# One matmul stream, eight column tiles: input scaled but not yet shifted, and w times shift added to the result

## The chip, the core and the metric

The kernel runs on one core of a Trainium2 chip. TensorE multiplies, VectorE (DVE), ScalarE (ACT) and GpSimd (POOL) do elementwise work, SyncE (SP) issues the loads, and 16 DMA engines carry them. The metric is device time of one execution in microseconds; the median of three executions of the kernel before is 2745.55 us.

## The reference, cut to what matters

The network is three transformer layers on 512 positions of width 2048. The change lies at the start of the first, where the input is normalised, scaled and shifted by vectors that depend on a condition `c`, and then multiplied by a wide matrix:

```python
sh_x, sc_x, gt_x = jnp.split((jax.nn.silu(c) @ w_ada[l] + b_ada[l])[:, None, :], 3, axis=-1)
h_x = rms_norm(x, norm_g[l]) * (1 + sc_x) + sh_x
h_c = rms_norm(hc, norm_g[l]) * (1 + sc_c) + sh_c
px = split_cols(h_x @ w_in[l])
pc = split_cols(h_c @ w_in[l])
```

`x` has 512 rows and the context `hc` 256. `w_ada` is 2048 x 6144 in float32: its scale and its shift third are 16.8 MB each. Everything is float32, and a product `h @ w` is made of three passes over operands that are split into a high and a low part.

## The kernel before

**Layout.** Activations stand transposed: 16 tiles of 128 features (k = 0 to 15) by 512 positions. One column tile of a weight is 128 output columns; it takes 16 x 3 matmuls of 128 x 512 (lines 491 to 493: high x high, high x low, low x high), and, where the context is projected too, 16 x 3 of 128 x 256 (496 to 498).

**The stream.** All weights go through one list of units of 256 KB, `self.units`, in the order in which TensorE uses them. A unit is either a quarter of a column tile (four k; called a quarter below) or one of 64 pieces of a third of `w_ada`. Two units make a pair, and a pair takes a slot of 512 KB. `loads` (in `stream`) issues a pair as soon as a slot of its kind is free. While the unit's number is below `EARLY` = 160, slots come from a ring of six (two `wr`, two `pt`, two pairs of `P`); after that from two `wr`. A quarter's unit is cast to the high part by ScalarE (line 554), the low part is the remainder, mostly by GpSimd (564); this uses the raw data up. A piece of `w_ada` is used raw: four pieces make a group of four matmuls on TensorE (667), and only when the group has run are their shares of the slots free. A slot is free when both of its units are used.

**The modulation stage (`block1`).** The pieces go by blocks of four k: the 16 pieces of the scale of block b, then the 16 of its shift. When a block's 16 pieces are in, its PSUM bank is copied (305 or 303), transposed by four small matmuls (641), and put into the table `modv` (647, 656). `make_h` then makes the four `hx` of that block: normalise by the row `rx` (772), scale and shift in one ScalarE instruction (786), cast (288), remainder (291). The first six column tiles are accumulated meanwhile in six PSUM places (`px` twice, `pc`, two halves of `S`, `O`): the quarter of block b of each of them stands in the list some pieces behind block b, with four pieces between two of them. When a tile is done, a query tile goes to `q_flow`, a gate tile to `silu`. Then the stream goes on with tiles that need the context too: key and value (A_T + 6, 7), key and value (8, 9), two more query tiles (10, 11), and so on.

**What sets the order.** Nothing is ordered by hand. `Sched` plans the instructions of all engines with a table of costs, and each engine then runs its list in that order, waiting for semaphores.

Of the kernel before, what the change touches and what calls it, by code (L numbers as in the profile page):

```python
# [12 lines left out]
AF = mybir.ActivationFunctionType  # L13
# [3 lines left out]
DRAM = bass.MemoryType.DRAM  # L17

KT = 16
EARLY = 160  # L20
LAG = (12, 4)
WAYS = 3
EARLY_OUT = ["px", "px", "pc"]
# [18 lines left out]
def f32(ap):  # L42
    return ap.bitcast(F32)
# [136 lines left out]
def D(n=0, x2=False, k=1, ptr=0):  # L180
    return ("DVE", k * (0.075 + n * (0.52e-3 if x2 else 1.04e-3) + 0.053 * ptr))
# [27 lines left out]
class Net:  # L209
    def __init__(self, ctx, tc, a, out):  # L210
        self.ctx, self.tc, self.nc, self.a, self.out = ctx, tc, tc.nc, a, out
        nc = tc.nc
        pool = lambda name, **kw: ctx.enter_context(tc.tile_pool(name=name, bufs=1, **kw))
        self.const, self.sb = pool("const"), pool("sb")
        self.ps, self.dram = pool("ps", space=PSUM), pool("dram", space=DRAM)
        self.s = Sched()
        self.tok = {k: Tok(v[1]) for k, v in {**SLOTS, **BANKS}.items()}
        self.uid = 0
        self.dma_free = 0.0
        self.units, self.marks = [], {}  # L220
# [3 lines left out]
        self.halves = c("halves", [128, 2])  # L224
# [279 lines left out]
    def stream(self):  # L504
# [9 lines left out]

        def ring(i):

            return (["wr"], ["pt"], ["P", "P"], ["wr"], ["pt"], ["P", "P"])[i // 2 % 6] if i < EARLY else ["wr"]

        def wring(i):
            return ("w", "act")[i % 2] if i < EARLY else "w"  # L520

        def loads():
            for i in range(0, len(self.units), 2):
# [102 lines left out]
    def ada_units(self, kind, b, tag="T"):  # L626
# [44 lines left out]
            return fn  # L671
        return [(blk[:, k * 512:(k + 1) * 512], None if k % 4 else four(k), True) for k in range(KT)], ev

    def gate(self):
# [82 lines left out]
        self.spawn(stats(), 3)  # L757
        return evs, fin

    def make_h(self, src, fin, n, row, w, mods, out, per):  # L760

        nc = self.nc
        left = [per] * (KT // per)
        slots = [Ev() for _ in range(KT)]

        def one(k):
            yield fin
            yield src[k]
            yield mods[k // 4]
            u = (yield from self.alloc("b"))[:, :n]  # L770
            e = yield [D(n), G(n)]
            (nc.gpsimd if e == "POOL" else nc.vector).tensor_tensor(u, src[k].val, row, op=OP.mult)
            left[k // per] -= 1
            if left[k // per] == 0:
                self.free("act")
# [9 lines left out]
            yield A(n, 2)  # L785
            nc.scalar.activation(u, u, AF.Identity, scale=self.modv[:, 1, k, w:w + 1], bias=self.modv[:, 0, k, w:w + 1])
            yield from self.split(hi, lo, u, pool=True)
            self.free("b")
            self.s.set(out[k], (hi, lo))
            done[0] -= 1  # L790
            if n == 256 and done[0] == 0:
                self.free("b")
        done = [KT]
        for k in range(KT):
            self.spawn(one(k), 2 if n == 512 else 3)


    def q_flow(self, px, free, out, gname, rope, scale):
# [197 lines left out]
    def attention(self, hd, spans, qk, post, qev, kev, vev, gev, k_out, free, sink=None, permute=False, prio=5):  # L996
# [78 lines left out]
        def pv_():  # L1075
            yield vev
            vloc, cs = vev.val, kev.val[1]
            for n, (t, ja, jb) in enumerate(tiles):
# [10 lines left out]
                mm(o, v[:, 1], pt[:, 0, :w], start=False, stop=n == 5, skip_group_check=True)  # L1089
                self.free("pt")  # L1090
            self.free(*free)
            yield gev
            th = gev.val
            o = yield from self.alloc("b", name="o")
# [124 lines left out]
    def block1(self):  # L1219
# [8 lines left out]
        ada = {}  # L1228
        mods = []
        for b in range(4):  # L1230
            s, e1 = self.ada_units(1, b)
            t, e0 = self.ada_units(0, b)
            both = Ev()

            def join(e0=e0, e1=e1, both=both):
                yield e0
                yield e1
                self.s.set(both)
            self.spawn(join())
            mods.append(both)  # L1240
            ada[b] = s + t
        st = {"n": 2}

        def half(i):
            def get():
# [7 lines left out]
            if st["n"] == 0:  # L1253
                self.free("S")
        fr = lambda t: (lambda: self.free(t))
        places = [("px", fr("px")), ("px", fr("px")), ("pc", fr("pc")), (half(0), freeS), (half(1), freeS), ("O", fr("O"))]
        q = {g: Ev() for g in range(4)}
        th = {g: Ev() for g in range(16)}
        sc128 = 128 ** -0.5
        first = []  # L1260
        for i, (tag, free) in enumerate(places):
            if i < 2:
                d = lambda px, pc, i=i, free=free: self.q_flow(px, free, q[i], "a_q_g", True, sc128)
            else:
                d = lambda px, pc, i=i, free=free: self.silu(px, free, th[i - 2])
            first.append(self.proj(w1[i], X, d, tag=tag))
# [3 lines left out]
        for n in range(len(flat) + 1):  # L1270
            U += [first[i][b] for m, b, i in todo if m == n or n == len(flat) <= m]
            U += flat[n:n + 1]
        xs, xfin = self.inputs(a["xT"], 512, self.rx, 2, *XMARK)

        def ctx():
            rc = (yield from self.alloc("b", name="rc"))[:, :256]
            cs, cfin = self.inputs(a["cT"], 256, rc, 4, *CMARK)
            self.make_h(cs, cfin, 256, rc, 1, mods, hc, 4)
        self.make_h(xs, xfin, 512, self.rx, 0, mods, hx, 2)
        self.spawn(ctx(), 3)  # L1280
        self.layer((14, 15))

        def add(t, flow, ctx=False):
            U.extend(self.proj(w1[t], X, flow, C if ctx else None))

        def kv(t, gname, rope, perm=False):
            kev, vev = Ev(), Ev()
# [12 lines left out]
        for n in range(2):  # L1300
            kev, vev = kv(t, "a_k_g", True)
            t += 2
            if n == 1:
                qt(t, q[2], "a_q_g", True)
                qt(t + 1, q[3], "a_q_g", True)
# [1071 lines left out]
```

## Time and profile before

| | |
|---|---|
| runs | 2740.39, 2745.55, 2749.77 us |
| profiled execution | 2743.26 us, of which 2741.2 us is the span from first to last instruction |
| TensorE busy | 2659.6 us (97%) |
| VectorE, ScalarE, GpSimd busy | 54%, 42%, 40% |
| DMA | 316 MB, mean 115 GB/s; 348 GB/s in the first fortieth of the span |

Times in the rows are from the span's start. A row of an engine's list gives its start, its duration, the line and the tiles (output <- inputs), and in brackets how long the engine had been idle and which instruction ended that. Matmuls overlap, so the distance between two starts tells their pace better than the duration. A full-precision matmul counts twice (x8 for four). `PEclk` or the granted clock is a share of TensorE's full 2.4 GHz.

### The profile page before, as it was taken

Reading aid. Unit: us, or ns where it says so; the run is one execution under the profiler, and the core shown is the slowest. Engines: PE = TensorE matmul, PEld = TensorE weight load, DVE = VectorE, ACT = ScalarE, POOL = GpSimd, SP = SyncE. Lnnn points to the kernel's source line nnn. Section 1 sums busy time; section 2 is a strip of 40 time slices with the busy share of each in tenths; the row PEclk is TensorE's granted clock in tenths of the full one; section 3 lists DMA queues with packets and bytes.
Section 4 is the critical chain, followed back from the end, with each engine's and each line's share of the span. In section 5 each row is a group of like instructions: output and inputs, shape, how many; then the busy total and the mean of one; then the engine's idle time right before and its main releaser. Section 6 shows DMA issues by size and latency. Waiting matters only on the chain.

```text
span 2741.2 us, 36539 instructions
## 1 busy us (share of the span) xinstructions
PE 2659.6 (97%) x13324; PEld 2189.9 (80%) x13324; DVE 1471.3 (54%) x3242; ACT 1164.1 (42%) x2361; POOL 1098.7 (40%) x886
## 2 busy tenths in 40 slices
PE   7889999999999999999999999999999999999999
PEld 3468888888888887788888878777888888888887
DVE  2457753336552656522368576765215877777500
ACT  3444433333332455433442445454334555555421
POOL 1351333334333333344445544445444333344544
PEclk8989999999999999999999999999999999999999
DMA  9845542222221213244222322224442222222443
GB/s 348 301 166 182 171 144 75 76 72 74 70 71 61 70 65 112 88 144 144 85 85 93 108 85 87 90 78 142 148 140 91 94 87 99 90 80 85 143 139 126
DMA packets 121960, 315.98 MB, mean 115 GB/s; under 512 B 13874, under 2 KB 23986, under 8 KB 121780
## 3 DMA queue, kind: packets, MB, share of 16 engines
q1 hardware_dynamic: 121780, 313.65, 34.4%
q8 instruction: 104, 1.70, 0.3%
q14 instruction: 76, 0.62, 0.1%
HBM read 293.02 MB, written 32.11 MB: 119 GB/s over the span
## 4 chain that ended last, share of the span: by engine, by line
PE 80%; DVE 13%; DMA 2%; ACT 2%; issue 1%; POOL 1%; SPq 0%; DVEq 0%; POOLq 0%; ACTq 0%
PE px L491 20%; PE px L492 20%; PE px L493 20%; PE T L398 4%; PE S L1113 2%; PE pc L496 1%; PE pc L498 1%; PE pc L497 1%; DVE P L1803 1%; DVE P L1815 1%; PE T L412 1%; DVE P L314 1%; PE O L1088 1%; PE O L1089 1%; DVE sm L1820 1%
## 5 line engine op out<-in xcount | busy, mean ns | idle before, releaser
L564 POOL TENSOR_TENSOR w<-wr,w 128x512 fp32r<-128x512 f32 x696 | 919.5, 1322 | 1423.1 <-ACT w L554 1419.0
L554 ACT ACTIVATE w<-wr 128x512 fp32r<-128x512 f32 x736 | 463.2, 630 | 948.4 <-PE px L493 616.0
L491 PE MATMUL px<-u,w 128*128 128x512 f32 x1248 | 498.5, 399 | 0.0
L492 PE MATMUL px<-u,w 128*128 128x512 f32 x1248 | 488.8, 392 | 0.0
L493 PE MATMUL px<-u,w 128*128 128x512 f32 x1248 | 488.4, 391 | 0.0
L491 PE MATMUL px<-hx,w 128*128 128x512 f32 x816 | 331.9, 407 | 9.4 <-ACT w L554 6.3
L492 PE MATMUL px<-hx,w 128*128 128x512 f32 x816 | 323.2, 396 | 2.2 <-POOL hx L291 2.2
L493 PE MATMUL px<-hx,w 128*128 128x512 f32 x816 | 322.3, 395 | 1.7 <-POOL w L564 1.7
L491 PE MATMUL px<-o,w 128*128 128x512 f32 x752 | 295.0, 392 | 3.3 <-ACT o L288 3.3
L492 PE MATMUL px<-o,w 128*128 128x512 f32 x752 | 294.3, 391 | 0.5 <-DVE o L291 0.5
L493 PE MATMUL px<-o,w 128*128 128x512 f32 x752 | 294.0, 391 | 0.0
L493 PEld LDWEIGHTS px<-u,w 128*128 128x128 f32 x1248 | 234.8, 188 | 51.3
L491 PEld LDWEIGHTS px<-u,w 128*128 128x128 f32 x1248 | 236.1, 189 | 40.7 <-issue 0.3
L492 PEld LDWEIGHTS px<-u,w 128*128 128x128 f32 x1248 | 235.7, 189 | 39.6
L291 DVE TENSOR_TENSOR pt<-T,pt 128x512 fp32r<-128x512 f32 (+2 forms) x208 | 127.0, 616 | 111.7 <-ACT pt L288 110.3
L493 PEld LDWEIGHTS px<-hx,w 128*128 128x128 f32 x816 | 154.9, 190 | 38.7 <-POOL w L564 3.3
L491 PEld LDWEIGHTS px<-hx,w 128*128 128x128 f32 x816 | 155.7, 191 | 32.9 <-ACT w L554 9.0
L492 PEld LDWEIGHTS px<-hx,w 128*128 128x128 f32 x816 | 155.7, 191 | 19.8 <-POOL hx L291 2.7
L491 PEld LDWEIGHTS px<-o,w 128*128 128x128 f32 x752 | 142.2, 189 | 33.4 <-ACT o L288 4.0
L492 PEld LDWEIGHTS px<-o,w 128*128 128x128 f32 x752 | 142.1, 189 | 30.5 <-DVE o L291 1.1
L493 PEld LDWEIGHTS px<-o,w 128*128 128x128 f32 x752 | 142.0, 189 | 29.3
L1598 DVE TENSOR_TENSOR xr<-px,xr 128x512 f32<-128x512 f32 x32 | 22.1, 692 | 251.0 <-PE px L493 248.1
(343 smaller groups left out, 4365.2 us busy)
## 6 DMA issues: line engine op xcount, KB each, us to landing
wr<-w SPq DMA_DIRECT2D x237, 512.0 KB, 3.5
wr<-wout SPq DMA_DIRECT2D x89, 512.0 KB, 4.2
wr<-wada SPq DMA_DIRECT2D x37, 512.0 KB, 6.8
gw<-wada SPq DMA_DIRECT2D x64, 256.0 KB, 5.3
wr<-w SPq DMA_DIRECT2D x58, 256.0 KB, 4.0
wr<-wada SPq DMA_DIRECT2D x54, 256.0 KB, 6.0
x<-xr SPq DMA_DIRECT2D x32, 256.0 KB, 4.3
xr<-x SPq DMA_DIRECT2D x32, 256.0 KB, 4.5
```

What stands on the lines that cost most here:

```text
L291: eng.tensor_tensor(lo, src, f32(hi), op=OP.subtract)
L314: self.nc.vector.tensor_scalar(dst, src, col, None, op0=OP.mult)
L398: self.nc.tensor.transpose(p[:, j * 128:(j + 1) * 128], x, self.ident)
L412: nc.tensor.matmul(p[:, j * gq:(j + 1) * gq], sq[:, j * 128:(j + 1) * 128], self.ones[:, 0:1] if gq == 1 else self.halves, start=True, sto ...
L491: mm(px, hi[:, s], x[0], **kw)
L492: mm(px, hi[:, s], x[1], start=False, stop=False)
L493: mm(px, lo[:, s], x[0], **ke)
L496: mm(pc, lo[:, s], c[0], **kw)
L497: mm(pc, hi[:, s], c[0], start=False, stop=False)
L554: nc.scalar.activation(w[:, 0], r, AF.Copy)
L564: (nc.gpsimd if e == "POOL" else nc.vector).tensor_tensor(w[:, 1], r, f32(w[:, 0]), op=OP.subtract)
L1113: self.nc.tensor.matmul(o, l, r, start=i == 0, stop=i == len(ops) - 1)
```

## The change

The stream now takes the scale of all four blocks first (64 pieces) and the shift of all four behind it. The first tiles use `h0`, the input scaled but not shifted, and there are eight of them: the two query tiles 10 and 11 join the six. Their PSUM result is copied to SBUF (`pre`) at once. The missing part, w transposed times shift, is one number for each output column: `off_units` loads each of the eight tiles' weights a second time, multiplies it by the shift column of `modv` (16 matmuls of one column), and ScalarE adds the result to `pre` before the tile's old flow goes on. These column sums stand one behind each quarter of the first key and value tile, in the order of tiles seven, eight, one to six. `shift_h` makes the shifted `hx` from `h0` for everything behind the eight tiles. The ring of slots becomes five pairs up to unit 136 (two `wr`, two `pt`, one pair of `p`), four up to 204, since `P` and `p` now hold `pre`. Context inputs take the fused scaling on VectorE and only the shift on ScalarE.

```diff
-EARLY = 160
+EARLY = 136, 204
 def ring(i):
-    return (["wr"], ["pt"], ["P", "P"], ["wr"], ["pt"], ["P", "P"])[i // 2 % 6] if i < EARLY else ["wr"]
+    if i < EARLY[0]:
+        return (["wr"], ["pt"], ["p", "p"], ["wr"], ["pt"])[i // 2 % 5]
+    return (["wr"], ["pt"])[i // 2 % 2] if i < EARLY[1] else ["wr"]
...
+def off_units(self, wt, i, shifted, ev):
...
+                for kk in range(4):
+                    k = u * 4 + kk
+                    nc.tensor.matmul(p[:, 0:1], raws[u][:, kk * 128:kk * 128 + 128], self.modv[:, 0, k, 0:1],
+                                     start=k == 0, stop=k == KT - 1)
...
 def make_h(...):
-            (nc.gpsimd if e == "POOL" else nc.vector).tensor_tensor(u, src[k].val, row, op=OP.mult)
+            nc.vector.scalar_tensor_tensor(u, src[k].val, self.modv[:, 1, k, w:w + 1], row, op0=OP.mult, op1=OP.mult)
-            nc.scalar.activation(u, u, AF.Identity, scale=self.modv[:, 1, k, w:w + 1], bias=self.modv[:, 0, k, w:w + 1])
+            if shifts is not None:
+                nc.scalar.activation(u, u, AF.Identity, bias=self.modv[:, 0, k, w:w + 1])
...
+def shift_h(self, old, shifts, new):
+            nc.vector.scalar_tensor_tensor(u, f32(hi), self.modv[:, 0, k, 0:1], f32(lo), op0=OP.add, op1=OP.add)
+            yield from self.split(s[:, 0], s[:, 1], u, pool=True)
...
 def block1(self):
+        def late(i, free, flow):
+                yield from self.copy(pre, px)
+                free()
+                yield off[i]
+                nc.scalar.activation(pre, pre, AF.Identity, bias=self.off[:, i:i + 1])
+                yield from flow(pre, fr(tag))
...
-        flat = [u for b in range(4) for u in ada[b]]
-        todo = [(32 * (b + 1) + LAG[0] + LAG[1] * i, b, i) for b in range(4) for i in range(len(places))]
+        flat = [u for b in range(4) for u in scale[b]]
+        todo = [(16 * (b + 1) + LAG[0] + LAG[1] * i, b, i) for b in range(4) for i in range(6)]
...
+        flat = [u for b in range(4) for u in shift[b]]
+        for n in range(0, 64, 4):
+            if n // 4 < len(rest):
+                U.append(rest[n // 4])
+            U += flat[n:n + 4]
+        U += rest[16:]
```

Three places of the engines' lists, before and now. First TensorE where the first projection begins; `T` is the bank of the modulation, `px` that of the first tile, L380 the norm row. Before:

```order
L380 MATMUL T_279<-b_269,ones 128x128 x4
L667 MATMUL T_204<-wr_210,cst 32x512
L667 MATMUL T_204<-wr_243,cst 32x512
L667 MATMUL T_204<-wr_248,cst 32x512 x2
L641 MATMUL T_303<-sel,b_298 128x2 x4
...
L667 MATMUL T_300<-wr_305,cst 32x512 x2
L491 MATMUL px_376<-hx_326,w_329 128x512
```

Now:

```order
L669 MATMUL T_214<-wr_232,cst 32x512 x2
L380 MATMUL T_276<-b_266,ones 128x128 x4
L491 MATMUL px_302<-hx_293,w_246 128x512
L492 MATMUL px_302<-hx_293,w_246 128x512
L493 MATMUL px_302<-hx_293,w_246 128x512
```

The first quarter now stands directly behind the norm row; before, 16 modulation matmuls and a transpose lay between.

Second SP, where a slot is reused; `wr_n` is a slot's filling, 128x1024 a pair in one load. Before, the pair `wr_346` has its slot (a `wr`) filled again six pairs later, and two other `wr` pairs stand in that ring:

```order
L540 DMA wr_346<-wada 128x512
L540 DMA wr_346<-w 128x512
L540 DMA wr_352<-wada 128x1024
L604 DMA cmask<-cmask 128x256
L540 DMA wr_354<-wada 128x512
L540 DMA wr_364<-wada 128x512
L540 DMA wr_369<-w 128x512
```

Now, in the shift stage, the pair `wr_716` is the fifth behind a pair of the same make, a weight and a piece, and takes its slot:

```order
L542 DMA wr_635<-wada 128x512
L542 DMA wr_635<-w 128x512
L742 DMA xt_644<-cT 128x1024
L542 DMA wr_676<-wada 128x1024
L542 DMA wr_685<-wada 128x512
L542 DMA wr_686<-wada 128x512
L542 DMA wr_716<-w 128x512
L542 DMA wr_716<-wada 128x512
```

The ring is one pair shorter, and every second weight of a quarter now shares the slot of the weight two quarters ahead of it.

Third TensorE behind the first quarter of the key tile, which reads `hx` and `w`. Before, the second quarter follows:

```order
L491 MATMUL px_1410<-hx_340,w_1225 128x512
L492 MATMUL px_1410<-hx_340,w_1225 128x512
L493 MATMUL px_1410<-hx_340,w_1225 128x512
L496 MATMUL pc_1411<-hc_972,w_1225 128x256
L497 MATMUL pc_1411<-hc_972,w_1225 128x256
L498 MATMUL pc_1411<-hc_972,w_1225 128x256
L491 MATMUL px_1410<-hx_567,w_1245 128x512
```

Now 16 one-column matmuls over raw weights stand between:

```order
L493 MATMUL px_1447<-hx_862,w_1386 128x512
...
L688 MATMUL T_1503<-modv,wr_1310 128x1 x4
L688 MATMUL T_1503<-modv,wr_1315 128x1 x8
L688 MATMUL T_1503<-modv,wr_1329 128x1 x4
L491 MATMUL px_1447<-hx_1010,w_1418 128x512
```

There are eight such groups, 128 matmuls, which is all that TensorE's list gains; nothing leaves it.

## Rows read from the trace of the kernel before

**Rows 1.** The page: span, and busy time of each engine.
```profile
span 2741.2 us, 36539 instructions
PE 2659.6 (97%) x13324; PEld 2189.9 (80%) x13324; DVE 1471.3 (54%) x3242; ACT 1164.1 (42%) x2361; POOL 1098.7 (40%) x886
```

**Rows 2.** Busy time by stretch, granted clock, DMA share and GB/s.
```profile
core 0: us, PE busy (x) PEld busy (x) DVE busy (x) ACT busy (x) POOL busy (x), PEclk, DMA share, GB/s
48.90:185.30 136.40, 117.66 (x533) 70.93 (x534) 63.44 (x130) 60.99 (x117) 63.45 (x54) 0.89 0.71 247
185.30:420.00 234.70, 232.48 (x1330) 200.14 (x1329) 153.55 (x290) 90.27 (x167) 65.59 (x53) 1.00 0.53 168
57.66:69.78 12.12, 12.10 (x62) 6.92 (x61) 0.42 (x4) 1.79 (x3) 2.57 (x2) 1.00 0.96 323
82.20:86.00 3.80, 3.13 (x8) 2.32 (x8) 1.13 (x1) 1.00 (x3) 1.84 (x2) 0.56 0.97 340
185.30:265.00 79.70, 79.44 (x470) 69.01 (x469) 50.23 (x99) 27.59 (x52) 15.10 (x11) 1.00 0.61 195
```

**Rows 3.** TensorE in order of time: first projection, one step, seventh tile.
```profile
48.94 0.50 PE L491 MATMUL px<-hx,w 128*128 128x512 f32 x1 [0.40 <-ACT w L554]
...
57.66 1.07 PE L667 MATMUL T<-wr,cst 128*32 128x512 f32 x8
58.65 0.50 PE L491 MATMUL pc<-hx,w 128*128 128x512 f32 x1
...
61.62 1.06 PE L667 MATMUL T<-wr,cst 128*32 128x512 f32 x8
...
185.27 0.39 PE L491 MATMUL px<-hx,w 128*128 128x512 f32 x1
185.50 0.39 PE L492 MATMUL px<-hx,w 128*128 128x512 f32 x1
```

**Rows 4.** SP's waits and weight loads in 49:74, then loads in 1500:1700.
```profile
SPq L540 <- PE T L667: 12.1, 5, 3.3
wr<-w SPq DMA_DIRECT2D x5, 256.0 KB, 5.0
wr<-w SPq DMA_DIRECT2D x4, 256.0 KB, 3.2
```

**Rows 5.** ScalarE in order of time: norm row, first weight's cast.
```profile
36.45 0.60 ACT L383 ACTIVATE rx<-T 128x512 f32<-128x512 f32 x1 [3.85 <-PE T L380]
...
48.26 0.63 ACT L554 ACTIVATE w<-wr 128x512 fp32r<-128x512 f32 x1 [2.20 <-DMA wr<-w]
```

**Rows 6.** TensorE's waits, 0:186: us in total, times, longest.
```profile
PE T L641 <- DVE b L305: 0.8, 1, 0.8
```

**Rows 7.** One weight from load to use: SP, ScalarE, GpSimd, TensorE.
```profile
59.13 0.43 SPq L540 DMA_DIRECT2D wr<-w  x1
65.27 0.63 ACT L554 ACTIVATE w<-wr 128x512 fp32r<-128x512 f32 x1 [4.98 <-DMA wr<-w]
65.98 1.28 POOL L564 TENSOR_TENSOR w<-wr,w 128x512 fp32r<-128x512 f32 x1 [4.31 <-ACT w L554]
67.31 0.50 PE L493 MATMUL S<-hx,w 128*128 128x512 f32 x1
```

**Rows 8.** TensorE's small matmuls, and a fused operation of VectorE.
```profile
164.85 0.94 PE L412 MATMUL T<-ones,b 128*128 128x1 f32 x8
165.66 0.49 PE L491 MATMUL pc<-hx,w 128*128 128x512 f32 x1
...
182.80 1.04 PE L1646 MATMUL T<-b,b 33*32 33x512 f32 x2
...
166.64 0.75 DVE L441 SCALAR_TENSOR_TENSOR b<-b,vec,rope 128x512 f32<-128x512 f32 x1
```

**Rows 9.** TensorE after its longest wait for a weight.
```profile
81.70 0.50 PE L491 MATMUL px<-hx,w 128*128 128x512 f32 x1 [3.21 <-ACT w L554]
...
84.13 0.63 PE L492 MATMUL px<-hx,w 128*128 128x512 f32 x1
84.55 0.63 PE L493 MATMUL px<-hx,w 128*128 128x512 f32 x1
```

More of the change, by code (lines that the diff above doesn't have):

```diff
@@ L672, in ada_units, with fn, out @@
         return [(blk[:, k * 512:(k + 1) * 512], None if k % 4 else four(k), True) for k in range(KT)], ev
+    def off_units(self, wt, i, shifted, ev):
+        nc = self.nc
+        def fn(raws):
+            for b in range(4):
+                yield shifted[b]
+            p = yield from self.alloc("T")
+            for u in range(4):
+                yield ("PE", 0.45)
+                for kk in range(4):
+                    k = u * 4 + kk
+                    nc.tensor.matmul(p[:, 0:1], raws[u][:, kk * 128:kk * 128 + 128], self.modv[:, 0, k, 0:1],
+                                     start=k == 0, stop=k == KT - 1)
+            def out():
+                yield D()
+                nc.vector.tensor_copy(self.off[:, i:i + 1], p[:, 0:1])
+                self.free("T")
+                self.s.set(ev)
+            self.spawn(out(), 2)
+        return [(wt[:, u * 512:(u + 1) * 512], None if u else fn, True) for u in range(4)]
     def gate(self):
@@ L758, in inputs, with make_h @@
         return evs, fin
-    def make_h(self, src, fin, n, row, w, mods, out, per):
+    def make_h(self, src, fin, n, row, w, scales, shifts, out, per):
         nc = self.nc
@@ L768, in one @@
             yield src[k]
-            yield mods[k // 4]
-            u = (yield from self.alloc("b"))[:, :n]
-            e = yield [D(n), G(n)]
-            (nc.gpsimd if e == "POOL" else nc.vector).tensor_tensor(u, src[k].val, row, op=OP.mult)
-            left[k // per] -= 1
-            if left[k // per] == 0:
-                self.free("act")
+            yield scales[k // 4]
+            if shifts is not None:
+                yield shifts[k // 4]
             if n == 512:
@@ L784, in one @@
                 hi, lo = s[:, k % 2, 0], s[:, k % 2, 1]
-            yield A(n, 2)
-            nc.scalar.activation(u, u, AF.Identity, scale=self.modv[:, 1, k, w:w + 1], bias=self.modv[:, 0, k, w:w + 1])
+            u = (yield from self.alloc("b"))[:, :n]
+            yield D(n, ptr=1)
+            nc.vector.scalar_tensor_tensor(u, src[k].val, self.modv[:, 1, k, w:w + 1], row, op0=OP.mult, op1=OP.mult)
+            left[k // per] -= 1
+            if left[k // per] == 0:
+                self.free("act")
+            if shifts is not None:
+                yield A(n, 1)
+                nc.scalar.activation(u, u, AF.Identity, bias=self.modv[:, 0, k, w:w + 1])
             yield from self.split(hi, lo, u, pool=True)
@@ L795, in make_h, with one @@
             self.spawn(one(k), 2 if n == 512 else 3)
+    def shift_h(self, old, shifts, new):
+        nc = self.nc
+        def one(k):
+            yield old[k]
+            yield shifts[k // 4]
+            s = yield from self.pair("hx")
+            u = yield from self.alloc("b")
+            hi, lo = old[k].val
+            yield D(512, ptr=1)
+            nc.vector.scalar_tensor_tensor(u, f32(hi), self.modv[:, 0, k, 0:1], f32(lo), op0=OP.add, op1=OP.add)
+            yield from self.split(s[:, 0], s[:, 1], u, pool=True)
+            self.free("b")
+            self.s.set(new[k], (s[:, 0], s[:, 1]))
+        for k in range(KT):
+            self.spawn(one(k), 2)
     def q_flow(self, px, free, out, gname, rope, scale):
@@ L1091, in pv_ @@
             self.free(*free)
+            if hd in self.gone:
+                self.s.set(self.gone[hd])
             yield gev
@@ L1226, in block1 @@
         X, C = (lambda k: hx[k]), (lambda k: hc[k])
[L1228 to L1242, printed above, removed]
+        scale, scaled = zip(*[self.ada_units(1, b) for b in range(4)])
+        shift, shifted = zip(*[self.ada_units(0, b) for b in range(4)])
+        h0 = [Ev() for _ in range(KT)]
+        X0 = lambda k: h0[k]
+        st = {"n": 2, "left": 8}
         def half(i):
@@ L1259, in block1, with done @@
         sc128 = 128 ** -0.5
-        first = []
+        cols = [A_T + i for i in (0, 1, 2, 3, 4, 5, 10, 11)]
+        first, offs = [], []
+        def late(i, free, flow):
+            def done(px, pc):
+                tag = ("P", "P", "P", "P", "P", "p", "b", "b")[i]
+                pre = (yield from self.alloc(tag, name="pre"))[:, :512]
+                yield from self.copy(pre, px)
+                free()
+                yield off[i]
+                yield A(512, 1)
+                nc.scalar.activation(pre, pre, AF.Identity, bias=self.off[:, i:i + 1])
+                if i > 5:
+                    yield self.gone[1]
+                yield from flow(pre, fr(tag))
+            return done
@@ L1261, in block1 @@
+        self.gone = {1: Ev()}
+        off = [Ev() for _ in cols]
         for i, (tag, free) in enumerate(places):
-            if i < 2:
-                d = lambda px, pc, i=i, free=free: self.q_flow(px, free, q[i], "a_q_g", True, sc128)
-            else:
-                d = lambda px, pc, i=i, free=free: self.silu(px, free, th[i - 2])
-            first.append(self.proj(w1[i], X, d, tag=tag))
-        flat = [u for b in range(4) for u in ada[b]]
-        todo = [(32 * (b + 1) + LAG[0] + LAG[1] * i, b, i) for b in range(4) for i in range(len(places))]
@@ L1270, in block1 @@
-        for n in range(len(flat) + 1):
-            U += [first[i][b] for m, b, i in todo if m == n or n == len(flat) <= m]
-            U += flat[n:n + 1]
+            g = {0: 0, 1: 1, 6: 2, 7: 3}.get(i)
+            if g is not None:
+                d = lambda px, free, g=g: self.q_flow(px, free, q[g], "a_q_g", True, sc128)
+            else:
+                d = lambda px, free, i=i: self.silu(px, free, th[i - 2])
+            first.append(self.proj(w1[cols[i]], X0, late(i, free, d), tag=tag))
@@ new lines, in block1, with last, g @@
+            offs.append(self.off_units(w1[cols[i]], i, shifted, off[i]))
+        offs = [offs[i] for i in (5, 4, 3, 2, 1, 0, 7, 6)]
+        def last(fn, u):
+            def g(hi, lo):
+                yield from fn(hi, lo)
+                self.free(*["act"] * 4)
+            return g
+        first[7] = [(x[0], last(x[1], u)) for u, x in enumerate(first[7])]
+        flat = [u for b in range(4) for u in scale[b]]
+        todo = [(16 * (b + 1) + LAG[0] + LAG[1] * i, b, i) for b in range(4) for i in range(6)]
@@ L1273, in block1 @@
+        for n in range(0, len(flat), 4):
+            U += [first[i][b] for m, b, i in todo if m == n]
+            U += flat[n:n + 4]
+        rest = [first[i][b] for m, b, i in todo if m >= len(flat)] + first[6] + first[7]
+        flat = [u for b in range(4) for u in shift[b]]
+        for n in range(0, 64, 4):
+            if n // 4 < len(rest):
+                U.append(rest[n // 4])
+            U += flat[n:n + 4]
+        U += rest[16:]
         xs, xfin = self.inputs(a["xT"], 512, self.rx, 2, *XMARK)
@@ L1277, in ctx @@
             cs, cfin = self.inputs(a["cT"], 256, rc, 4, *CMARK)
-            self.make_h(cs, cfin, 256, rc, 1, mods, hc, 4)
-        self.make_h(xs, xfin, 512, self.rx, 0, mods, hx, 2)
+            self.make_h(cs, cfin, 256, rc, 1, scaled, shifted, hc, 4)
+        self.make_h(xs, xfin, 512, self.rx, 0, scaled, None, h0, 2)
+        self.shift_h(h0, shifted, hx)
         self.spawn(ctx(), 3)
@@ L1283, in add @@
         def add(t, flow, ctx=False):
-            U.extend(self.proj(w1[t], X, flow, C if ctx else None))
+            for u in self.proj(w1[t], X, flow, C if ctx else None):
+                U.append(u)
+                if offs:
+                    U.extend(offs.pop())
         def kv(t, gname, rope, perm=False):
```

10 lines of the change are left out of this document (4 added, 6 removed).

## The prediction, made before the changed kernel ran

> **What bounds the kernel now.** I read the page first. TensorE is busy 97% of the span [rows 1], so only its own work or its idle time can move the end. The same sums by stretch show where idle time is left [rows 2]: from 48.9 to 185.3 us TensorE works 117.7 of 136.4 at a granted clock of 0.89, and from 185.3 to 420 us 232.5 of 234.7 at 1.00. The change lies in the first 185 us, the modulation stage, so I read that stage in TensorE's order of time. The first projection starts as late as 48.94, and the seventh column tile, the first that also reads the context, at 185.27 [rows 3]. Six tiles are done by then; after it TensorE hardly waits. The end therefore moves by the difference in when this dense stretch begins, plus the work that is moved across its start.
>
> Between those two times a step of the stream is one group of four modulation matmuls and one projection quarter (12 matmuls). At full clock it takes 3.96 us: 57.66 to 61.62 [rows 3]. DMA is 0.96 busy then and TensorE 12.10 of 12.12 us [rows 2], so the two are level; SP itself spends 12.1 us of that quarter waiting for modulation matmuls to give a slot back [rows 4]. That says which resource is tight: slots, more than bytes.
>
> **The start.** Before, the first quarter comes behind scale and shift of block 0, and last waits for its own weights, cast at 48.26 [rows 5]. Now it needs only the scale and the norm row, and its weight is the 29th piece of the stream instead of the 45th. The norm row is cast at 36.45 for 0.60 us [rows 5]; I leave that time, since the x tiles are moved by less than 1 us of transfer. Then VectorE does four scalings of 0.75 (the nearest fused form [rows 8]) and three remainders. These I take at 0.65 as an estimate, a little under the fused form: 37.1 + 3.0 + 2.0 = 42.1. Queued starts overlap a little, two more matmuls follow: 42.
>
> **TensorE's work until eight tiles are done.** After that first quarter the new order has 31 quarters, 25 groups of four, seven modulation transposes and the context norm. 25 steps x 3.96 = 99.0. Six quarters without a group x 12 x 0.23 = 16.4. Seven transposes of as many passes as the one-column group [rows 8], 0.81 each, = 5.7. Norm about 1. Sum 122, ending at 164 if nothing waits.
>
> **What waits in there.** Two kinds. (1) Four shift blocks end with the transpose directly behind the last group, so TensorE waits for the copy of the bank: 0.8 each [rows 6], 3.4 with the semaphores. (2) Slots. The ring falls from six pair slots to five, and to four from piece 136. A pair that holds a quarter's weight and a modulation piece comes free only when its group of four has run, and in a ring of five it is reused by the weight of the quarter after next. The chain from there [rows 7]: the group ends at 58.65, SP issues, the weight lands after 6.1 us (59.13 to 65.2), ScalarE casts (65.27), GpSimd's remainder runs 65.98 to 67.26, and the third matmul of the quarter runs at 67.31. Cast and remainder take 2.1 us. In the ring of six this refill is due two steps later (7.9 us) and is just in time. In the ring of five, every second step, it is due one step later: 2.97 + 0.99 + 0.57 to the third matmul = 4.5 us. With the latency of a quiet stretch (1500 to 1700 us), 3.2 us [rows 4], the chain is 5.4 and the wait 0.9. With 5.0, the median of the opening [rows 4], it is 7.2 and the wait 2.7. I count eight such places: five bare, three where a transpose and its copy give 1.7 us more. Low 5, high 18. In the ring of four, modulation pieces too are due 2.97 us after their slot is free, against 3.2 to 5.0 and the issue: 2.5 to 7.5 us over four steps with the weights that follow them. With the copies: 11 to 29 us. The new stretch would draw some 1.31 MB a step in 4.5 us, about 290 GB/s, not far from the opening's 323 [rows 2], but with fewer loads in flight; I take a latency of 4.0, between the two rows, and 16 us. Eight tiles are then done at 42 + 122 + 16 = 180.
>
> The rows show a 256 KB load landing in 3.2 us in the quiet stretch and in 5.0 in the opening [rows 4]. The Trainium skill (DMA: Bandwidth & Descriptors, "Latency and other measured facts") states that a lighter HBM load makes a transfer's fixed cost smaller; the trace agrees. Carried to the end, the waits here would be 11 us and the eighth tile done at 175. The same page ("Rules for kernel authors") wants a DMA issued early so that its setup cost is covered; the ring of five does the opposite, and by that rule the higher sum, 193, is due.
>
> **What is moved across.** Behind 185.27 the old kernel still had tiles seven and eight of these (two query tiles): 96 matmuls x 0.2275 = 21.8 us that leave. Added behind: eight column sums w times shift, each 16 matmuls of one column with full-precision weights. The trace has this form, four at 0.81 us (164.85 to 165.66 [rows 8]): 8 x (3.24 + 0.1) = 26.7. Also two table products of 1.04 [rows 8] and two groups of query sums of 0.81, which ran before 185.27 and now run behind it: 3.7. Net +8.6. The eight tiles' second load from memory, 8.4 MB, is hidden: this stretch uses 0.61 of the DMA time [rows 2], and a step there has 7.4 us. If that cover failed it would be a refill wait again. The shifted inputs cost VectorE 16 x 0.75 and remainders, ScalarE 16 casts, under the eighth tile (11 us) and the first two context tiles (8 quarters x 7.4); only their first part is close. I charge 1.5 us, between 0 and 6.
>
> **Sum.** 180 + 8.6 - 185.3 + 1.5 = +4.8. The profiled execution took 2743.3 us (span 2741.2 [rows 1], 2.1 around it): 2748. The median of the runs shown is 2745.6, 2.3 above the profiled one.
>
> **Rivals.** (a) The refills are in time: SP issues at once, loads return in 3.2 us, and part of the rest lies under transposes. Then only copies and a little of the ring of four wait, some 4 us: 168 + 8.6 - 185.3 = -9, 2734. For it: TensorE has work in hand at block boundaries, where it now idles up to 3.2 us [rows 9]. Against: the ring of six has already no slack [rows 7]. (b) Slower: the refill behind the group of four sets the pace of the shift stage. At a latency of 5.0, 29 us of waits, eight tiles at 193, +17. The clock adds to it: after a wait of 3.21 us matmuls run 0.42 apart instead of 0.23 [rows 3, 9], for eight of them, and the granted clock of that stretch is 0.56, mostly the lower level, 1.2 GHz [rows 2]; at 1.6 us for each of three longer waits, +22: 2765. It decides from a latency of about 4.5 us on. The Trainium skill (TensorE: Matmul & The Clock Gate, "HAM oscillation") warns of such gaps in a matmul stream. (c) Slower, later: two query flows, four gates, the second shift and the rest of the context, some 36 us of VectorE work, come into the stretch from 185 to 265, where it is busy 50 of 80 us [rows 2]. If attention then waits on it, about +8 on top: 2756.
>
> **Chances.** Forecast (within 8 us) 0.42; (a) 0.25; (b) 0.23; (c) 0.10. About 0.3%, 8.2 us, is what a measurement of this kernel can tell from no change. Case (a) is faster by that, (b) and (c) slower, the forecast same. The range, 2733 to 2764, holds (a)'s centre and most of (b).
>
> **What would show it.** The first quarter at 38 to 42 us with no shift before it. In the shift stage, third matmuls of every second quarter that wait for GpSimd's remainder, and the copies' 0.8 four times; if these waits sum to under 5, (a); over 25, (b). The eighth tile's end near 180. One-column groups at 3.3 us a tile. If the first context tile idles for shifted inputs, or attention for VectorE, the 1.5 us are wrong. A first quarter as late as 48 would void the whole sum.

## The result and the profile after

The changed kernel took 2785.71 us (median of four runs, 2782.20 to 2793.55), the one before 2747.66 beside it: a ratio of 1.0145, 95% interval 1.0114 to 1.0177. It is slower by 38 us. The forecast was 2748 and its range ended at 2764. The profiled execution took 2786.48, with a span of 2784.7, 43.5 more than before. All sums below are made on that pair of spans.

The page of the changed kernel (line numbers are its own):

```profile
span 2784.7 us, 37174 instructions
PE 2704.1 (97%) x13580; PEld 2232.4 (80%) x13580; DVE 1508.2 (54%) x3288; ACT 1162.9 (42%) x2367; POOL 1116.3 (40%) x890
```

TensorE is as full as before, 97% [rows 1], and that is the first thing to learn here: a busy share tells nothing of the clock at which the work was done. The same sums by stretch, with the granted clock as the third number from the end:

```profile
48.40:196.00 147.60, 131.57 (x640) 80.61 (x640) 66.48 (x112) 49.23 (x95) 70.71 (x51) 0.97 0.74 251
199.00:285.00 86.00, 86.00 (x500) 76.85 (x499) 50.84 (x100) 32.15 (x63) 24.26 (x20) 0.80 0.65 215
300.00:420.00 120.00, 116.69 (x651) 100.49 (x650) 92.22 (x179) 45.41 (x89) 33.45 (x24) 0.96 0.54 168
```

From 199 to 285 us, where the column sums stand, TensorE has no idle time at all and a clock of 0.80; before, it was 1.00 there [rows 2]. That is 86 x 0.20 = 17.2 us of full speed lost in a stretch without one wait. TensorE in order of time shows where, around the first of the eight sums:

```profile
199.52 3.63 PE L688 MATMUL T<-modv,wr 128*128 128x1 f32 x32
203.01 0.48 PE L491 MATMUL px<-hx,w 128*128 128x512 f32 x1
...
204.67 0.63 PE L493 MATMUL px<-hx,w 128*128 128x512 f32 x1
...
208.02 0.39 PE L492 MATMUL px<-hx,w 128*128 128x512 f32 x1
...
208.82 4.53 PE L688 MATMUL T<-modv,wr 128*128 128x1 f32 x32
```

A sum's 16 products (two records each, so x32) take 3.49 us from their start to the next matmul. The matmuls behind them run at the full 2.4 GHz (0.39 to 0.40 us each) for 1.4 us, then at 1.2 GHz (0.63) for about 3.4 us, and then at 2.4 GHz again (0.39 at 208.02). The next group begins at full clock too, but the clock falls inside it, and it takes 4.53. All eight groups are not alike: behind four of them there is one such spell, behind three a longer one, and behind the sixth, at 254.16, none.

The other part of the loss lies ahead of it. The first quarter, selected rows of ScalarE, then VectorE, then TensorE:

```profile
38.69 0.60 ACT L383 ACTIVATE rx<-T 128x512 f32<-128x512 f32 x1 [1.66 <-PE T L380]
39.32 3.75 DVE L808 SCALAR_TENSOR_TENSOR b<-xt,modv,rx 128x512 f32<-128x512 f32 x4 [3.12 <-ACT rx L383]
42.99 2.97 DVE L291 TENSOR_TENSOR hx<-b,hx 128x512 fp32r<-128x512 f32 x3
40.78 0.80 PE L491 MATMUL px<-hx,w 128*128 128x512 f32 x1 [2.13 <-ACT hx L288]
...
44.81 0.79 PE L492 MATMUL px<-hx,w 128*128 128x512 f32 x1 [0.59 <-DVE hx L291]
...
47.97 0.63 PE L493 MATMUL px<-hx,w 128*128 128x512 f32 x1
```

The quarter is done at 48.4, not 42. The norm row comes 2.2 us later than before [rows 5], the scalings take 0.94 and the remainders 0.99 each, and the matmuls run at half clock. TensorE's largest waits between 48.9 and 185 us (total, times, longest):

```profile
PE T L391 <- DVE b L769: 3.3, 1, 3.3
PE T L643 <- DVE b L305: 2.7, 3, 0.9
PE px L493 <- POOL w L566: 2.1, 3, 0.9
PE T L380 <- DVE b L376: 1.7, 1, 1.7
PE pc L493 <- POOL w L566: 1.7, 1, 1.7
PE S L493 <- POOL w L566: 1.6, 3, 0.8
```

The first context tile, that is, the first column tile that is multiplied with the context too, starts at 195.3 (at 185.27 before [rows 3]); its first product with the context:

```profile
196.02 0.28 PE L496 MATMUL pc<-hc,w 128*128 128x256 f32 x1
```

**The account of the 43.5 us.** The context tiles start 10.1 later. The moved work is -21.8 + 3.7, as forecast (not measured apart). The sums cost 8 x 3.49 = 27.9 at full clock and 17.2 of clock. From 300 to 420 the clock of 0.96 costs 4.8, and idle time is 3.3 in place of 2.0. Together 10.1 - 18.1 + 45.1 + 6.1 = 43.2. The last term comes almost wholly from one wait, the only one that the list has from 285 to 420 us: TensorE waits for a copy that VectorE makes of a key tile, and the clock is low behind it.

```profile
PE T L398 <- DVE p L903: 3.2, 1, 3.2
360.00:380.00 20.00, 17.70 (x80) 15.54 (x81) 14.87 (x41) 5.85 (x12) 2.59 (x2) 0.74 0.40 116
```

That the account closes to 0.3 us is in part luck. The norm row of the second layer shows how far the kernels are apart by then, before and now:

```profile
874.12 1.05 PE L380 MATMUL T<-b,ones 128*128 128x128 f32 x8
915.48 1.06 PE L380 MATMUL T<-b,ones 128*128 128x128 f32 x8
```

They are 41.4 apart there, and 2.1 more come later.

### The profile page after: what moved, and what is told of

Its sections match the earlier page's. It is cut to its first block, busy times and chain, and to the rows that moved or that the text cites. A ratio compares the mean times of both kernels' runs of the same rounds, so it can differ in the third digit from the quotient of the medians.

```text
span 2784.7 us, 37174 instructions
## 1 busy us (share of the span) xinstructions
PE 2704.1 (97%) x13580; PEld 2232.4 (80%) x13580; DVE 1508.2 (54%) x3288; ACT 1162.9 (42%) x2367; POOL 1116.3 (40%) x890
## 4 chain that ended last, share of the span: by engine, by line
PE 80%; DVE 13%; DMA 2%; issue 2%; ACT 1%; POOL 1%; SPq 1%; POOLq 0%; ACTq 0%; DVEq 0%
PE px L491 20%; PE px L492 19%; PE px L493 19%; PE T L398 4%; PE S L1161 2%; PE pc L496 1%; PE pc L497 1%; PE pc L498 1%; DVE P L1879 1%; PE T L688 1%; DVE P L1891 1%; PE T L412 1%; PE T L669 1%; POOL w L566 1%; PE O L1134 1%
## 5 line engine op out<-in xcount | busy, mean ns | idle before, releaser
L288 ACT ACTIVATE pt<-T 128x512 fp32r<-128x512 f32 (+2 forms) x208 | 109.7, 535 | 118.0 <-PE O L1135 72.3
```

Source lines behind the costliest of these rows:

```text
L288: nc.scalar.activation(hi, src, AF.Copy)
```

## The experiments

Theory: the narrow products lower TensorE's clock behind them, and a late first quarter is carried on to the context tiles. Rivals: the clock falls for something else that is new there, the second load costs time, or VectorE is late. The letters A, B and so on are those of the expectation that stands above each result.

Executions of one kernel lie up to 14 us apart, and the medians of the kernel before, timed again beside each set of runs, went from 2741.2 to 2747.7. A difference of a few us between two runs shows little by itself. Each ratio below is to the kernel before in the same set; a difference from the changed kernel is one of medians from different sets. Where it matters I compare traces over the same work, from the first product with the context to the norm row of the second layer: 185.95 to 874.12, 688.2 us, in the kernel before, and 196.02 to 915.48, 719.5, in the changed one.

**1. The sums all but left out.**

```
+                    if k not in (0, KT - 1):
+                        continue
                     nc.tensor.matmul(p[:, 0:1], raws[u]...
```

> The changed kernel with 2 of the 16 one-column products of each column sum left (14 of 16 are left out; all loads stay). Base: the changed kernel's profiled 2786.5 us, where the 128 products are busy 31.2 us and the granted clock of the stretch 199 to 285 us is 0.80, which is 86 x 0.20 = 17 us of full speed lost, against 1.00 before. Theory A (the one-column groups lower the clock of the matmuls behind them): 27 us of their own and nearly all of the 17 go, about 2744 us, and the clock in the first two context tiles is 1.00. Rival B (the clock falls for something else that is new in that stretch: the second load, VectorE's crowd, the narrow context matmuls): only the 27 go, about 2759 us, and the clock stays near 0.8. Rival C (the products hide a VectorE lag that shows once they go): 2765 us or more, with TensorE idle for shifted inputs.

Measured 2766.09 (ratio to before 1.0082, 1.0067 to 1.0097). That is 20 less than the changed kernel, or 14 if each is set against the kernel before beside it.

```profile
200.00:260.00 60.00, 46.99 (x243) 37.77 (x242) 45.43 (x90) 27.54 (x55) 20.02 (x18) 0.89 0.75 255
260.00:320.00 60.00, 60.00 (x360) 52.30 (x359) 46.23 (x87) 25.54 (x48) 17.15 (x13) 1.00 0.61 186
```

C met the time, and it came on top of A: the clock of 260 to 320 is 1.00 again, but TensorE now idles 13 us between 200 and 260, with a clock of 0.89. The products had lain over waits. These are not the waits that C named: none is for a shifted input. The two largest are 3.5 us for casts of weights on ScalarE and 3.0 for a remainder of the context input on VectorE.

**2. The products alone, on the kernel before.** In that kernel's `proj`, behind each quarter of its first two context tiles:

```
+                    for k in range(KT):
+                        mm(p[:, 0:1], self.ident, self.ident[:, k:k + 1], start=k == 0, stop=k == KT - 1)
```

> The kernel before with eight groups of 16 one-column products added, one behind each quarter of its first two context tiles, on data that is there already (no loads, no other edit; what they compute is not used). Before: 2743.3 us profiled, granted clock 1.00 behind 185 us. Theory A: 8 x 3.6 = 29 us of their own and some 15 of lowered clock behind them: about 2787 us, clock near 0.8 in the two tiles. Rival B: their own time alone, 2772 us, clock 1.00.

Measured 2786.61 (1.0163, 1.0142 to 1.0184). The form on TensorE, and the stretch:

```profile
L505 PE MATMUL T<-ident 128*128 128x1 f32 x256 | 29.8, 250 | 0.0
185.00:320.00 135.00, 133.70 (x818) 119.99 (x817) 64.62 (x130) 35.52 (x67) 21.63 (x16) 0.91 0.45 146
```

Theory A: the same fall of the clock, without a load, a shifted input or a new order. It is smaller, 135 x 0.09 = 12 us. With the products' own 29.8 that makes 41.8.

**3. The same products, 128 columns wide.**

```
-                        mm(p[:, 0:1], self.ident, self.ident[:, k:k + 1], start...
+                        mm(p[:, 0:128], self.ident, self.ident, start...
```

> The kernel before with the same eight groups of 16 products as in the run with one-column products on it, now 128 columns wide in place of one (what they compute is not used). With one column they were busy 29.8 us and the whole took 2782.0 profiled, the clock behind 185 us 0.77 to 0.97. Theory A (it is the narrow products that are followed by the lower clock): clock 1.00 from 185 to 320, the products' own time between 30 us (if the weight load sets their pace, as its 0.19 us a row suggests) and 55, so 2773 to 2798 us with no half-clock matmuls behind them. Rival B (any stretch of products with such weight loads does it): clock as low as with one column, 2785 us or more.

Measured 2779.24 (1.0127, 1.0111 to 1.0143).

```profile
L505 PE MATMUL T<-ident 128*128 128x128 f32 x256 | 29.9, 275 | 0.0
185.00:320.00 135.00, 133.64 (x864) 119.06 (x864) 70.33 (x138) 38.51 (x72) 23.99 (x18) 1.00 0.48 157
```

Theory A in its plainest form: 128 times the columns, the same 29.9 us, and the clock stays at 1.00. The time moved by 7 us and not by 12, and the two intervals touch. The trace says where the 12 are. First product with the context and norm row (line 381 in these kernels), run 2 and then this run:

```profile
183.81 0.28 PE L497 MATMUL pc<-hc,w 128*128 128x256 f32 x1
913.79 1.05 PE L381 MATMUL T<-b,ones 128*128 128x128 f32 x8
188.44 0.28 PE L497 MATMUL pc<-hc,w 128*128 128x256 f32 x1
906.58 1.05 PE L381 MATMUL T<-b,ones 128*128 128x128 f32 x8
```

The same work takes 730.0 us with one column and 718.1 with 128, against 688.2 without the products: 41.8 and 30.0 more, the products' own time with and without the loss of clock. The profiled executions end closer together because this run's start was 4.6 us later and the rest of the program behind the norm row took 5.5 us longer; why was not looked into.

**4. The changed kernel's own sums made wide.** The shift column is repeated, so the sum is the same in each of 128 columns:

```
-                    nc.tensor.matmul(p[:, 0:1], raws[u]..., self.modv[:, 0, k, 0:1],
+                    nc.tensor.matmul(p[:, 0:128], raws[u]..., self.modv[:, 0, k, 0:1].to_broadcast([128, 128]),
```

> The changed kernel with each one-column product made 128 columns wide by repeating the shift column (the sum is the same, in every column); nothing left out. Theory A: the granted clock of 199 to 285 us goes from 0.80 to near 1.00, which takes up to 17 us away, less what VectorE's lateness then shows, 2769 to 2778 us. Rival B (clock not a matter of the width): 2786 us or more.

Measured 2773.16 (1.0107, 1.0090 to 1.0124), 12.6 less than the changed kernel, or 6.7 if each is set against the kernel before beside it. The stretch, and the two ends of the compared work:

```profile
L688 PE MATMUL T<-modv,wr 128*128 128x128 f32 x256 | 30.0, 273 | 0.0
199.00:285.00 86.00, 83.62 (x572) 74.61 (x572) 58.70 (x113) 36.23 (x70) 26.07 (x21) 1.00 0.69 221
194.99 0.28 PE L496 MATMUL pc<-hc,w 128*128 128x256 f32 x1
901.20 1.05 PE L380 MATMUL T<-b,ones 128*128 128x128 f32 x8
```

The clock is back and 2.4 us of idle time show instead. The same work takes 706.2 us, 13.3 less than in the changed kernel. With run 3 this settles the cause of the low clock: the width of the products, not their place, the loads or the time that they take.

**5. The products dealt out in fours.** Three of the eight sums are held and run inside the next quarter:

```
+                    if self.part:
+                        yield from self.part(kk)
...
+            if i in (1, 2, 3, 4, 5):
+                for u in range(4):
+                    yield from part(u)
+            else:
+                self.part = part
```

> The changed kernel with the first three of the eight column sums spread: their 16 products run in four fours, each behind three projection and three context matmuls of the next quarter; the other five as before. Nothing is left out. Theory A1 (a run of 16 one-column products in one piece is what lowers the clock): no fall around the first three, clock 1.00 from 199 to about 232 us instead of 0.79, falls only behind the other five; some 7 us less, 2779 us. Rival A2 (the sum of one-column work in the stretch counts, however it is dealt out): clock as low as in the changed kernel, 2786 us.

Measured 2814.91, one execution. Both missed, on the same side. The stretch of the first spread sum, and one that holds the other two:

```profile
202.30:210.90 8.60, 7.08 (x52) 6.38 (x50) 8.60 (x12) 5.69 (x14) 5.72 (x6) 1.00 0.00 0
230.00:260.00 30.00, 27.71 (x111) 24.96 (x110) 6.88 (x12) 4.72 (x8) 1.78 (x2) 0.50 0.55 178
```

Around the first, four fours from 202.3 to 210.9, the clock stayed at 1.00, as A1 had it. Then TensorE waited 3.2 and 4.8 us, and the clock fell. The other two spread sums, between 226 and 255 us, came behind these waits, and 30 us pass at half clock without a break. So the fours did not lower the clock here; it stayed low while they went on among full matmuls. Some 10 us of idle time from 199 to 230 are part of the price; that the spread sums hold slots and a bank longer may be why. One execution with both effects in it can't tell them apart.

**6. Each sum as four 512-column products, a copy and four picks.**

```
+                nc.tensor.matmul(p[u * 32:u * 32 + 32], <32 columns of shift>, raws[u], start=True, stop=True, ...)
+                yield from self.copy(r, p)
+                    nc.tensor.matmul(p[:, 0:1], r[:, kk * 128:...], self.sel32[:, 2 * kk:2 * kk + 1], ...)
```

> The changed kernel with each column sum computed as four products 512 columns wide (the raw weight moves, 32 columns of shift stand), a copy and four one-column picks, in place of 16 one-column products. Nothing is left out. A four of 512-column products takes 1.06 us in the changed kernel's rows and four one-column ones 0.95, so 2.0 a sum in place of 3.9: 15 us less. Theory A: the clock stays at 1.00 as well, 17 us more: about 2754 us. Rival B: the clock stays low, about 2771 us. Either way the start is as in the changed kernel, the eighth tile done at 196 us.

(The table of the picks, `sel32`, is made once the first block's shift is there.) Measured 2779.36 (1.0128, 1.0103 to 1.0153; 2771.8 to 2785.5, a wide scatter). In the profiled execution, the fastest, TensorE's own time for the sums fell from 31.2 to 18.1 us and the clock from 199 to 285 us was 0.92, but the picks wait for the copy on VectorE:

```profile
PE T L708 <- DVE b L306: 7.7, 3, 6.5
```

Neither number was met by the median. What the run shows is that work given back to VectorE in this stretch comes late.

**7. Neither load nor sums.** Two products a sum, on resident data, and no second load:

```
-EARLY = 136, 204
+EARLY = 136, 172
...
-                    nc.tensor.matmul(p[:, 0:1], raws[u]...
+                    if k not in (0, KT - 1):
+                        continue
+                    nc.tensor.matmul(p[:, 0:1], self.ident, self.modv[:, 0, k, 0:1],
...
-                    U.extend(offs.pop())
+                    self.behind[len(U) - 1] = offs.pop()[0][1]
```

The ring's second bound moves because 32 units are gone.

> The changed kernel without the second load of the eight tiles' weights, and with 2 of 16 products of each sum, on data that is there already (the sums are left out). The run with two products and the load took 2764.6 profiled and idled about 13 us between 200 and 260 us. Theory A (what it still paid is the second load: it takes slots and DMA from the context tiles' own weights): these waits go, under 4 us of idle between 200 and 320, about 2748 us. Rival B (the waits are VectorE's, which is late with the shifted inputs and the eight tiles' second halves): they stay, about 2763 us.

Measured 2764.76 (1.0085, 1.0070 to 1.0100): within 2 us of run 1, so B. The load was not what run 1 paid. One stretch, TensorE's largest wait in it, SP's largest from 205 to 216 us, and VectorE's largest group from 185 to 215:

```profile
200.00:320.00 120.00, 108.04 (x608) 90.53 (x607) 88.81 (x178) 57.70 (x111) 32.39 (x26) 0.94 0.51 158
```
```profile
PE T L1727 <- DMA b<-onehot: 6.1, 1, 6.1
SPq L542 <- POOL w L566: 10.7, 1, 10.7
```
```profile
L840 DVE SCALAR_TENSOR_TENSOR b<-hx,modv 128x512 f32<-128x512 f32 x8 | 12.1, 1582 | 0.0
```

The wait named a DMA is for a table's load that SP issued only at 210.87. SP's list shows why: a weight's load in front of it waited 10.7 us for its slot, until a remainder on GpSimd ended at 209.6. The cast that this remainder needs ran at 207.55 on ScalarE, behind context inputs that had waited for VectorE's scalings. VectorE itself is busy 27.8 of the 30 us from 185 to 215; its eight shift additions take 1.58 us each there, against the 0.75 reckoned with.

**8. All sums, no second load.** As run 7, with all 16 products of a sum.

> The changed kernel without the second load, its eight sums with all 16 products on data that is there already (what they compute is not the sum). Theory A (beside the one-column products the second load costs nothing, it lies under them): 2783 to 2787 us and the clock low again, near 0.8, behind 200 us. Rival B (the load adds to the products' price): some 2770 us.

Measured 2789.85 (1.0176, 1.0160 to 1.0191), profiled 2787.23 beside the changed kernel's 2786.48; the clock from 199 to 285 us is 0.79. A: no gain shows from leaving the second load out. A few us could be hidden, since the first context product came 4.5 us later here (200.5 against 196.0). With run 7, the 14 products a sum that differ cost 25 us net, 4 of them by that start, though they and the clock weigh some 40: the rest lies over waits.

**9. Run 7 without the shifted inputs.**

```
-        X0 = lambda k: h0[k]
+        X = X0 = lambda k: h0[k]
...
-        self.shift_h(h0, shifted, hx)
```

> The run without sums and without the second load once more, now also without the shifted inputs: later tiles read the scaled input (the shift is left out of all of them). It takes 16 fused additions, 16 casts and 16 remainders away, most of them between 180 and 215 us, where VectorE was busy 15 of 15 us. The run it is compared with took 2763.8 profiled and idled 12 us on TensorE between 200 and 320. Theory A (making the shifted inputs under the eighth tile puts VectorE behind, and the context tiles wait for what it does late): the idle time falls under 4 us and the clock there comes to 1.00, 2748 us or less. Rival B (VectorE is late because the eight tiles' second halves, two query flows more, stand there): idle stays above 8 us, 2760 us.

Measured 2754.01 (1.0040, 1.0027 to 1.0053), 10.8 less than run 7:

```profile
200.00:320.00 120.00, 114.05 (x675) 98.88 (x674) 92.54 (x175) 52.05 (x95) 31.33 (x23) 0.97 0.56 176
```

Idle time falls from 12.0 to 6.0. Between A and B: the shifted inputs are about half of the idle time; the rest was not taken apart.

**10. No row norm of x.**

```
+        if n == 512:
+            self.nc.vector.memset(row, 1.0)
+            self.s.set(fin)
+            return evs, fin
```

> The changed kernel without the row norm of x (its squares, sums and row are left out; the scaled input is made with a row of ones), so the first projection quarter waits for its scale and weight alone. In the changed kernel the norm's row was ready about 39 us, the first quarter ran from 40.8 to 48.4 us where the prediction had it done at 42, and the first context tile started at 196.0. Theory A (from then on TensorE's own work and waits follow one another, so the late first quarter is carried on in full): the first quarter is done some 4 to 8 us earlier, the context tiles start at 188 to 192 and the whole takes 2779 to 2782 us. Rival B (the loads, through the ring of slots, set the pace behind it): the context tiles start at 194 or later, 2784 us or more.

Measured 2777.83 (1.0122, 1.0098 to 1.0147), 7.9 less than the changed kernel. The first quarter's first and last matmul, and the first context products (first and last start, count, shape):

```profile
36.29 0.50 PE L491 MATMUL px<-hx,w 128*128 128x512 f32 x1 [0.29 <-ACT w L556]
...
39.92 0.39 PE L493 MATMUL px<-hx,w 128*128 128x512 f32 x1
```
```profile
L496 PE MATMUL pc<-hc,w x12: 274/278/415, 186.6 to 208.6; 128*128 128x256 f32 x12
```

A: the quarter is done 8.2 us earlier, the context starts 9.4 earlier. The loads keep up; a late start is carried on in full to the context tiles.

**11. The context norm put first.**

```
-            self.spawn(squares(i), 3)
-        self.spawn(stats(), 3)
+            self.spawn(squares(i), 3 if n == 512 else 1)
+        self.spawn(stats(), 3 if n == 512 else 1)
```

> The changed kernel with the context norm's squares and sums put ahead of the shifted inputs in the planner's priorities (1 in place of 3); nothing else. In the changed kernel TensorE waits 3.3 and 1.7 us for them near 145 to 152 us and then works 4 us at half clock. Theory A (the norm's lateness is part of why eight tiles were done at 196 us and not at 180): 5 us of waits and some 2 of clock go, eighth tile done at about 189, 2779 us. Rival B (what stands behind it on VectorE is late instead): within 3 us of 2786.

Measured 2791.76 (1.0177, 1.0159 to 1.0195): not better, so B in sign, and nothing gained. The waits only fell from 5.0 to 4.1 us, and the first context product came at 202.2, 6.2 later than in the changed kernel: the clock from 48 to 202 us was 0.93 in place of 0.97. Why is open, so this says little of what the waits cost.

**12. Four pairs from piece 64.**

```
-            if i < EARLY[0]:
+            if i < 64:
```

> The changed kernel with the ring of five pairs cut to four from piece 64 on, where it was from piece 136; nothing left out. Theory A (the refills bind as the prediction had it: in a ring of four every piece is due about 3 us after its slot is free, and takes 4 to 6): 1.5 us or more in each of some 18 steps, 27 us or more, 2813 us. Rival B (the loads have slack, the ring hardly binds): under 6 us, 2786 to 2792.

Measured 2798.34 (1.0212, 1.0195 to 1.0229), 12.6 more than the changed kernel by the medians and 8.1 by the profiled executions; the first context product came at 205.9, 9.9 later. The two largest of its refill waits, which sum to 17.6 us (7.1 in the changed kernel):

```profile
PE S L493 <- POOL w L566: 5.8, 5, 3.0
PE px L493 <- POOL w L566: 5.7, 6, 2.9
```

Between the two: a ring shorter by a pair costs 10 us over 18 steps, 0.55 a step. The mechanism is right, and its size a third of the 1.5 us a step expected of this run. The prediction had 2.5 to 7.5 us over four steps of such a ring, 0.6 to 1.9 a step.

No run is faster than the kernel before. The wide sums and the early first quarter (runs 4 and 10) add up to 2785.7 - 12.6 - 7.9 = 2765 at best, an estimate that was not run, and run 10 leaves work out.

## Why the prediction was wrong

**The step that failed most** is "8 x (3.24 + 0.1) = 26.7" behind 185 us. The products' own time was nearly right, 27.9. The price of what they do to the matmuls behind them had no term: 17.2 us. Rows 8 have only short runs of that form with full matmuls at 0.49 right behind, and I read the clock of 1.00 in [rows 2] as a property of the stretch, though it belonged to the work in it. Rival (b) had the clock, but behind waits and in the shift stage. The Trainium skill (TensorE: Matmul & The Clock Gate, "HAM oscillation"), which the prediction cites there, puts the fall of the clock down to gaps between matmuls; in this trace it fell in a stretch with 86.00 us busy of 86.00.

**"The first quarter done at 42"** was 48.4, and the prediction itself had said that 48 would void its sum. Each of its parts was put at its best: the norm row unmoved (2.2 us later, since its products stand behind a transpose and modulation groups at half clock), 0.75 and 0.65 for operations that took 0.94 and 0.99, and 0.23 for matmuls that ran 0.43 apart. Run 10 shows that such a delay is carried on: 8.2 us earlier here were 9.4 at the context tiles and 7.9 at the end.

**"Eight tiles are then done at 180"** was 195.3: 6.4 from the first quarter and 8.9 of TensorE's busy time, 130.9 where I had 122. Of these 4.4 are a clock of 0.97, 1.9 two groups (at 58.4 and 169.8, at full clock) that took 2.0 us in place of 1.06; 2.6 stay open.

**The waits of 16 us** were 16.0, and that is luck. Copies: 3.7 (3.4 forecast; 1.0 of it the list puts to ScalarE). Refills: 7.1, not 12.6; GpSimd's remainders are 5.4 of it and casts 1.7. The context norm made up for it: 5.0 of waits, where the sum had 1 us of work and no wait.

**The second load at nothing** held as far as run 8 can tell. **VectorE at 1.5 us** was too low. Up to 300 us the sums cover its lateness: with two products in place of 16, 12 to 13 us of idle time show (runs 1 and 7), of which the shifted inputs are about half (run 9). Behind 300 the cover ends, and the one wait for VectorE there, 3.2 us with 20 x 0.26 = 5.2 of clock around it, costs 8.4. That is the size of rival (c), at the copy of a key tile and not in attention; why VectorE was late for it was not taken apart.

**The sum:** 38.7 us above the forecast's +4.8, of which 15.3 by 195.3 us, 18.4 from the sums and their clock, and 4.6 from 300 to 420; 0.4 is left over.

## What to carry to other kernels

Price a group of narrow matmuls by its own time and by the clock of what follows it, and look at the granted clock of a stretch, not at the busy share, to see it; where only a column is wanted, repeating it to 128 columns cost no time of its own here and kept the clock. Added work on a full engine may lie over another engine's lateness, so taking it away gives back less than it weighs. A stage whose steps follow one another without slack carries a late start to its end: reckon its first step with the slow rows, not the best ones.

## What was not expected of the hardware

Products of one column and of 128 took the same time with the same weight loads: 29.8 and 29.9 us for 128 of them, but the granted clock over 135 us was 0.91 with the one and 1.00 with the other. In run 5 one-column products were mixed into full matmuls: behind waits of 3.2 and 4.8 us the clock stayed at 0.50 for 30 us, with TensorE busy 27.7 of them, while around the first such sum, ahead of the waits, it was 1.00.
